# A gated recurrence block on one core: mirrored groups of keys in every second chunk, and the recurrence's last steps behind the bank adds

## The chip, the cores and the metric

The kernel runs on one core of a Trainium2 chip. The metric is the device time of one execution in microseconds, the median of several runs. The engines are named as in the profile: PE is TensorE, DVE is VectorE, ACT is ScalarE, POOL is GpSimd, SP is SyncE, which issues most of the DMAs.

## The reference, cut to what matters

One decoder block on 1024 tokens of width 1024 in float32. A projection gives the queries, the forget gates f, the values, output gates, a pooling branch and merge gates. The part that the change touches is the recurrence, with 8 heads of width 128:

```python
# S_t = diag(f_t) S_{t-1} + k_t v_t^T,  o_t = S_t^T q_t,  k_t = 1 - f_t
scores = einsum('td,sd->ts', q_dec, k_inv);  scores = where(causal, scores, 0)
o_intra = einsum('ts,sv->tv', scores, v)
o_inter = einsum('td,dv->tv', q_dec, state)
state   = decay * state + einsum('sd,sv->dv', k_to_end, v)
```

Its output is normed, gated and projected, merged with the pooling branch, and two layer norms and a squared-ReLU MLP follow. The sum over key tokens s stands in `o_intra` and in the new state, so an order of the keys changes neither, as long as scores, values and decayed keys have the same one.

## The kernel before, in words

All large products are built from 512 x 512 blocks. `pair` computes one block of weights against both token halves with seven products in place of eight (p1 to p7); each product is 12 matmuls of 512 columns (`prod`: high and low parts of weights and activations, lines 213, 215 and 216) into a PSUM bank `ps_pj`. A finished bank is copied out by ACT (`copied`, line 294) or added to an earlier result by DVE (`added`, line 298, the **bank add**). A bank serves a later product only when it has been read. The weights of each product are split into two parts by ACT (line 250) and DVE (line 251).

The tokens of a head are worked in two halves of 512 tokens, and a half in 4 chunks of 128 tokens. A half (`Half`) goes through `prepare` (DVE, ACT and POOL: cumulative decays by scans, then queries and keys scaled in several ways), `turn_keys` (transposes of the decayed keys `ke`, tile `tC`), `scores`, `far_queries`, `states` and `outputs`. `recurrence` is a generator that runs these steps, one or a few between two products of the projections: `PER_HALF` = 8.25 products to a half. The order of TensorE's instructions is thus written by hand; the orders of DVE, ACT, POOL and SP are made by a scheduler that plans with estimated times, so that they can shift wherever an instruction or an order edge changes. `issue_after` puts the instructions of a `with` block behind a named instruction of the same engine.

`scores` fills the tile `sc`, 128 key tokens (partitions) by 4 x 128 query tokens. A chunk's keys stand in four groups of 32, and every matmul has 32 keys as its weights, so it writes 32 partitions: group b writes partitions 32b to 32b + 31, here called quarter 32b. There are three kinds: 4 **diagonal** matmuls to a chunk (`sc<-tF,tD`, 32 columns), 2 **near** ones (`sc<-q,tE`, groups 2 and 0 against the next group of queries, 32 columns) and 2 **far** ones (`sc<-q,k`, groups 0 and 1 against the last 64 queries). The far ones read `q64` and `k64`, each of which is half an ACT copy (lines 1057 and 1060) and half a DVE product (lines 1058 and 1061). The causal part of `sc` is copied into `att` under the mask `cmask` (line 1089). The other DVE steps of `prepare` that the text names are `q` and `tE` by `T` (lines 1049 and 1050) and `ke`, which is `tC<-tE,ek` (line 1052).

The values are computed early and stored to DRAM by `put` (line 554), 128 tokens by 512 columns at a time; `values` loads them for each half.

Of the kernel before, what the change touches and what calls it, by code (L numbers as in the profile page):

```python
# [22 lines left out]
HALF = 512  # L23
CH = HALF // P
SUB = 16
NB = HALF // SUB
# [26 lines left out]
def tile_hybrid_block(  # L53
# [18 lines left out]
    nc = tc.nc  # L72
    V, A, G, PE = nc.vector, nc.scalar, nc.gpsimd, nc.tensor
# [5 lines left out]
    const = ctx.enter_context(tc.tile_pool(name="const", bufs=1))  # L79
# [51 lines left out]
    def split_into(t, src):  # L131
# [3 lines left out]

    ident = const.tile([P, P], F32, name="ident")
    make_identity(nc, ident)
    cmask = const.tile([P, P], F32, name="cmask")
    G.memset(cmask, 1.0)
    G.affine_select(  # L140
        out=cmask, in_=cmask, compare_op=ALU.is_ge, fill=0.0, base=0,
        pattern=[[1, P]], channel_multiplier=-1,
    )
# [99 lines left out]
    def w_tile():  # L243
        return wq.tile([P, CH, P], F32R, tag="w", name=nm("w"), bufs=NW)

    hi_of, lo_of, last_act = [], [], [None]

    def w_part(src):
        hi, lo = w_tile(), w_tile()
# [13 lines left out]

    def behind_act():
        return tc.issue_after(last_act[0])

    n_c = [0]

# [17 lines left out]
    def pair(raw, rooms, takes, pz_tag="pj", twin=False, pc_tag="pj", turned=False):  # L286


        b11, b12, b21, b22, t = raw if len(raw) == 5 else (*raw, None)
        c, ps = {}, {}  # L290

        def copied(room, ps):
            t = room()
            noted(A.copy(t, ps))  # L294
            return t

        def added(t, ps):
            V.tensor_add(t, t, ps)  # L298
            return t

        def make_t3():
            c["t"] = block_tile() if t is None else t
            V.tensor_sub(c["t"], b22, b12)  # L303

        def t3():
            if twin:
                make_t3()
            return w_part(c["t"])

        def t2():  # L310
            if not twin:
                make_t3()
                make_t2()
            return w_part(b12)

        def make_t2():
            if turned:
                minus_sum(b12, c["t"], b11)
            else:
                V.tensor_add(b12, c["t"], b11)  # L320

        def t4():
            if twin:
                make_t2()
            if turned:
                minus_sum(b21, b12, b21)
            else:
                V.tensor_sub(b21, b21, b12)
            return w_part(b21)

        def t1():
            if turned:
                minus_sum(c["t"], b22, b12)
            else:
                V.tensor_sub(c["t"], b22, b12)
            return w_part(c["t"])

        def p1(w):
            ps["a"] = ps_tile()
            prod(ps["a"], w, "a11", True)  # L340
            c[11] = copied(rooms[0], ps["a"])

        def p2(w):
            if pz_tag == "pj":
                ps["z"] = ps_tile()
            ps["c"] = ps_tile(pc_tag, 4 if pc_tag == "pj" else 2)
            prod(ps["c"], w, "a12", True)

        def p7(w):
            if pz_tag != "pj":  # L350
                ps["z"] = ps_tile(pz_tag, 2)
            prod(ps["z"], w, "s3", True)
            with tc.high_priority(PRIO):
                takes[0](added(c[11], ps["c"]))
                c[22] = copied(rooms[2], ps["z"])

        def p6(w):
            prod(ps["a"], w, "s2", False)
            with tc.high_priority(PRIO):
                c[21] = copied(rooms[1], ps["a"])  # L360
                if twin:
                    takes[2](added(c[21], ps["z"]))

        def p4(w):
            prod(ps["z"], w, "a22", False)
            if not twin:
                with tc.high_priority(PRIO):
                    takes[2](added(c[21], ps["z"]))

        def p5(w):  # L370
            prod(ps["a"], w, "s1", False)
            with tc.high_priority(PRIO):
                takes[3](added(c[22], ps["a"]))

        def p3(w):
            prod(ps["a"], w, "s4", False)
# [81 lines left out]
    vd = [[dram(f"v{u}_{nh}", CH * HALF) for nh in range(2)] for u in range(2)]  # L458
    ca = ctx.enter_context(tc.tile_pool(name="ca", bufs=4, reuse_waits="tile"))
    wq = w_scope.enter_context(tc.tile_pool(name="wq", bufs=1, side="right", reuse_waits="tile"))  # L460
    with tc.tile_pool(name="xr", bufs=8, side="right", reuse_waits="tile") as xr:
# [5 lines left out]
        ps = ps_tile("hg", 2)  # L467
# [83 lines left out]
                    take(c, ps)  # L551

        def put(u, nh, c, t):
            nc.sync.dma_start(out=vd[u][nh].rearrange("p (c d) -> p c d", d=HALF)[:, c], in_=t)

        c11, c21, c22 = ([None] * CH for _ in range(3))
        taken = {}
# [184 lines left out]
    with tc.tile_pool(name="tmp", bufs=1, side="right", reuse_waits="tile") as tmp:  # L742
# [227 lines left out]
        def pairs_of(t):  # L970
            return t.rearrange("p (b e s) -> p b e s", e=2, s=SUB)

        def half64(t, e):
            return t.rearrange("p (c e b s) -> p c e b s", e=2, b=2, s=2 * SUB)[:, :, e]

        def bc(a, shape):
            return a.unsqueeze(len(a.shape)).to_broadcast(shape)

        def chunk(c):
            return slice(c * P, (c + 1) * P)  # L980

        def b32(t):
            return t.rearrange("p (b s) -> p b s", s=32)

        class Half:
# [4 lines left out]
            def prepare(self):  # L990

                h, u = self.h, self.u
# [15 lines left out]
                rT = small("rT", [P, NB])  # L1008
                V.reciprocal(rT, blk(fd)[:, :, SUB - 1])
                rT2 = rT.rearrange("p (b e) -> p b e", e=2)  # L1010
                T = small("T", [P, NB])
# [21 lines left out]
                V.tensor_mul(q, q, fd)  # L1033
                k = ft
                with behind_act():
                    A.activation(k, ft, AF.Identity, bias=cmask[:, P - 1 : P], scale=-1.0)
                self.kr = kr = tt("tE")
                V.tensor_mul(kr, k, to_end)
                yield
# [9 lines left out]
                V.tensor_mul(pairs_of(q)[:, :, 1], pairs_of(q)[:, :, 1], bc(T2[:, :, 0], [P, NB // 2, SUB]))  # L1049
                V.tensor_mul(pairs_of(kr)[:, :, 0], pairs_of(kr)[:, :, 0], bc(T2[:, :, 1], [P, NB // 2, SUB]))  # L1050
                self.ke = ke = to_end
                V.tensor_mul(b32(ke), b32(kr), bc(ek.rearrange("p c b -> p (c b)"), [P, 16, 32]))
                yield
                self.q64 = q64 = hgp.tile([P, CH, 2, 32], F32, tag="q64", name=nm("q64"))
                self.k64 = k64 = hgp.tile([P, CH, 2, 32], F32, tag="k64", name=nm("k64"))
                with behind_act():
                    A.copy(q64[:, :, 0], half64(q, 1)[:, :, 0])
                V.tensor_mul(q64[:, :, 1], half64(q, 1)[:, :, 1], bc(p32[:, :, 2], [P, CH, 32]))
                with behind_act():
                    A.copy(k64[:, :, 1], half64(kr, 0)[:, :, 1])  # L1060
                V.tensor_mul(k64[:, :, 0], half64(kr, 0)[:, :, 0], bc(p32[:, :, 1], [P, CH, 32]))
                self.q = q

            def turn_keys(self):
# [8 lines left out]
            def scores(self):  # L1073

                def score(part, lo, keys, queries):
                    PE.matmul(sc[part : part + 32, lo : lo + queries.shape[-1]], keys, queries, start=True, stop=True)
# [12 lines left out]
                V.copy_predicated(  # L1089
                    att, cmask.bitcast(U32).unsqueeze(1).to_broadcast([P, CH, P]),  # L1090
                    sc.rearrange("p (c t) -> p c t", t=P),
                )

            def far_queries(self):
# [565 lines left out]
```

## Time and profile before

| | |
|---|---|
| median of 3 runs | 1442.57 us (1440.68 to 1442.67) |
| profiled execution | 1440.68 us; span from first to last instruction 1439.0 us |
| granted TensorE clock | 0.998 |
| busy: PE, DVE, ACT, POOL | 1424.9, 1099.3, 753.6, 108.6 us |
| blocks of scores (tile `sc`) | 16, the first at 136.8 us, the last until 547 us |
| mean DMA traffic | 159 GB/s |

In rows of the timeline the columns are start in us, length in us, engine, line, operation, output<-inputs, shape and count; what ended an idle time before the row stands in brackets. A row by tile gives the shortest, median and longest duration in ns. Matmuls overlap, so their lengths are not to be summed: what counts is the step from one start to the next.

### The profile page before, as it was taken

The numbers are of one execution on the slowest core, as the hardware profiler recorded it, in microseconds if no ns is written. First come the engines' busy times: TensorE is split into PE (matmuls) and PEld (weight loads), VectorE is DVE, ScalarE is ACT, GpSimd is POOL, SyncE is SP. The second block draws the span as 40 slices with busy tenths as digits, with TensorE's granted clock in tenths as the row PEclk, the third lists the DMA queues.
The fourth block names the chain that finished last, engine by engine and source line by source line (L and its number), as shares of the span: only waits on it lengthen the run. The fifth ranks groups of instructions, "written<-read, shape, count | busy, mean of one in ns | idle before, by whom it ended". The sixth has DMA issues, their size and how long they took to land.

```text
span 1439.0 us, 21137 instructions
## 1 busy us (share of the span) xinstructions
PE 1424.9 (99%) x7499; PEld 1184.6 (82%) x7499; DVE 1099.3 (76%) x1816; ACT 753.6 (52%) x1376; POOL 108.6 (8%) x296
## 2 busy tenths in 40 slices
PE   9999999999999999999999999999999999999997
PEld 7888888888888888878888888888888888888886
DVE  5967887897797796579965697666666787777978
ACT  5445566666656655456532375555556443433534
POOL 0002011111211210100003000000000100000000
PEclk9999999999999999999999999999999999999999
DMA  7142254444454546799651225444456864444422
GB/s 271 62 137 91 87 131 148 109 128 145 110 125 132 142 124 189 214 325 348 190 205 64 99 66 189 155 161 161 149 180 245 292 243 146 149 141 167 133 73 117
DMA packets 186794, 228.17 MB, mean 159 GB/s; under 512 B 12192, under 2 KB 110784, under 8 KB 186688
## 3 DMA queue, kind: packets, MB, share of 16 engines
q1 hardware_dynamic: 180080, 210.94, 44.0%
q0 software_dynamic: 5824, 13.63, 4.5%
q10 hardware_dynamic: 784, 2.25, 0.5%
q8 instruction: 59, 0.97, 0.3%
q14 instruction: 47, 0.39, 0.1%
HBM read 149.70 MB, written 77.07 MB: 158 GB/s over the span
## 4 chain that ended last, share of the span: by engine, by line
PE 94%; DVE 3%; DMA 1%; issue 1%; ACT 1%; DVEq 0%; POOL 0%; ACTq 0%; SPq 0%; POOLq 0%
PE ps_pj L213 16%; PE ps_pj L215 16%; PE ps_pj L216 16%; PE ps_pj L1539 4%; PE ps_pj L1538 4%; PE ps_pj L1537 4%; PE ps_pj L115 2%; PE ps_pj L116 2%; PE ps_pj L114 2%; PE ps_tr L1539 2%; PE ps_tr L1538 2%; PE ps_tr L1537 2%; PE ps_hg L216 1%; PE ps_sc L213 1%; PE ps_sc L216 1%; PE ps_hg L213 1%
## 5 line engine op out<-in xcount | busy, mean ns | idle before, releaser
L213 PE MATMUL ps_pj<-act,w 128*128 128x512 f32 x1068 | 420.1, 393 | 2.7 <-DVE c L298 2.4
L215 PE MATMUL ps_pj<-act,w 128*128 128x512 f32 x1068 | 415.4, 389 | 0.0
L216 PE MATMUL ps_pj<-act,w 128*128 128x512 f32 x1068 | 415.1, 389 | 0.0
L250 ACT CAST w<-raw 128x512 fp32r<-128x512 f32 x303 | 187.7, 621 | 260.6 <-PE ps_pj L215 179.9
L251 DVE TENSOR_TENSOR w<-raw,w 128x512 fp32r<-128x512 f32 x303 | 207.1, 686 | 95.8 <-ACT w L250 93.3
L213 PEld LDWEIGHTS ps_pj<-act,w 128*128 128x128 f32 x1068 | 200.6, 188 | 46.1 <-DVE c L298 3.7
L216 PEld LDWEIGHTS ps_pj<-act,w 128*128 128x128 f32 x1068 | 200.5, 188 | 42.2
L215 PEld LDWEIGHTS ps_pj<-act,w 128*128 128x128 f32 x1068 | 200.6, 188 | 40.4
L1499 ACT CAST act<-act 128x1024 fp32r<-128x1024 f32 x66 | 67.1, 1050 | 108.4 <-issue 35.0
L1538 PE MATMUL ps_pj<-act,act 128*128 128x512 f32 x240 | 93.1, 389 | 0.0
L1539 PE MATMUL ps_pj<-act,act 128*128 128x512 f32 x240 | 93.1, 389 | 0.0
L1500 DVE TENSOR_TENSOR act<-act,act 128x1024 fp32r<-128x1024 f32 x66 | 79.4, 1219 | 17.4 <-ACT act L1499 17.4
L1537 PE MATMUL ps_pj<-act,act 128*128 128x512 f32 x240 | 92.6, 389 | 0.0
L298 DVE TENSOR_TENSOR c<-c,ps_pj 128x512 f32<-128x512 f32 x91 | 62.1, 683 | 33.4 <-PE ps_pj L216 32.3
L294 ACT COPY c<-ps_pj 128x512 f32<-128x512 f32 x92 | 53.3, 581 | 3.3 <-PE ps_pj L216 1.8
L1538 PEld LDWEIGHTS ps_pj<-act,act 128*128 128x128 f32 x240 | 45.1, 188 | 9.5 <-DVE act L1500 0.2
L1537 PEld LDWEIGHTS ps_pj<-act,act 128*128 128x128 f32 x240 | 45.1, 188 | 9.4
L1539 PEld LDWEIGHTS ps_pj<-act,act 128*128 128x128 f32 x240 | 45.1, 188 | 9.3
L303 DVE TENSOR_TENSOR raw<-raw,raw 128x512 f32<-128x512 f32 x43 | 29.6, 688 | 24.6 <-DMA raw<-in_w_in_dram 19.7
L1408 ACT ACTIVATE c<-c 128x512 f32<-128x512 f32 x61 | 38.5, 633 | 1.7
L1407 ACT ACTIVATE c<-c 128x512 f32<-128x512 f32 x46 | 29.0, 632 | 16.3 <-DVE c L298 16.3
L737 POOL DMA_DIRECT2D s<-og x28 | 24.9, 1162 | 137.1 <-DVE og L1150 137.1
(432 smaller groups left out, 2706.4 us busy)
## 6 DMA issues: line engine op xcount, KB each, us to landing
h<-c SPq DMA_DIRECT2D x106, 256.0 KB, 2.9
raw<-in_w_in_dram SPq DMA_DIRECT2D x100, 256.0 KB, 3.3
act<-h SPq DMA_DIRECT2D x78, 256.0 KB, 2.9
draw<-in_w_down_dram SPq DMA_DIRECT2D x16, 1024.0 KB, 8.2
raw<-in_w_up_dram SPq DMA_DIRECT2D x56, 256.0 KB, 2.9
hf<-h SPq DMA_DIRECT2D x34, 256.0 KB, 2.9
s<-og POOLq DMA_DIRECT2D x28, 256.0 KB, 6.0
v<-v SPq DMA_DIRECT2D x16, 256.0 KB, 3.4
```

Source lines behind the costliest of these rows:

```text
L213: PE.matmul(ps, wh[:, k], th, start=first and k == 0, stop=False, skip_group_check=True)
L215: PE.matmul(ps, wh[:, k], tl, start=False, stop=False, skip_group_check=True)
L216: PE.matmul(ps, wl[:, k], th, start=False, stop=k == CH - 1, skip_group_check=True)
L250: hi_of.append(A.copy(hi, src).ins)
L251: lo_of.append(V.tensor_sub(lo, src, f(hi)).ins)
L294: noted(A.copy(t, ps))
L298: V.tensor_add(t, t, ps)
L1499: A.copy(hi, src)
L1500: V.tensor_sub(lo, src, f(hi))
L1537: PE.matmul(ps, hh[:, w], wh, start=fresh and n == 0, stop=False, skip_group_check=True)
L1538: PE.matmul(ps, hh[:, w], wl, start=False, stop=False, skip_group_check=True)
L1539: PE.matmul(ps, hl[:, w], wh, start=False, stop=n == M - 1, skip_group_check=True)
```

## The change

The keys of chunks 1 and 3 of each half stand in mirrored order of their four groups of 32 (3, 2, 1, 0). Three places follow suit: the quarter of `sc` that a group's matmul writes (`place`), the values in DRAM (`put` stores an odd chunk by four DMAs of 32 tokens), and `ke`, which is now made by one DVE instruction for the even chunks and one, with reversed groups, for the odd ones. `cmask` gets a second mask for the odd chunks. In `scores` all near matmuls now come ahead of all far ones. Two small tiles, `rT` and `T`, have one buffer and not two. And in `prepare` the DVE steps on `q`, `kr` (`tE`), `ke`, `q64` and `k64` are put behind the latest bank add (`behind_add`).

```diff
-    cmask = const.tile([P, P], F32, name="cmask")
+    cmask = const.tile([P, 2, P], F32, name="cmask")
     G.memset(cmask, 1.0)
...
+    for b in range(4):
+        part = cmask[b * 32 : (b + 1) * 32, 1]
+        G.affine_select(
+            out=part, in_=part, compare_op=ALU.is_ge, fill=0.0, base=-32 * (3 - b),
+            pattern=[[1, P]], channel_multiplier=-1,
+        )
...
+    def behind_add():
+        return tc.issue_after(last_add[0])
...
         def added(t, ps):
-            V.tensor_add(t, t, ps)
+            last_add[0] = V.tensor_add(t, t, ps).ins
             return t
...
         def put(u, nh, c, t):
-            nc.sync.dma_start(out=vd[u][nh].rearrange("p (c d) -> p c d", d=HALF)[:, c], in_=t)
+            to = vd[u][nh].rearrange("p (c d) -> p c d", d=HALF)[:, c]
+            if c % 2 == 0:
+                nc.sync.dma_start(out=to, in_=t)
+            else:
+                for b in range(4):
+                    nc.sync.dma_start(out=to[(3 - b) * 32 : (4 - b) * 32], in_=t[b * 32 : (b + 1) * 32])
...
-                V.tensor_mul(pairs_of(q)[:, :, 1], pairs_of(q)[:, :, 1], bc(T2[:, :, 0], [P, NB // 2, SUB]))
-                V.tensor_mul(pairs_of(kr)[:, :, 0], pairs_of(kr)[:, :, 0], bc(T2[:, :, 1], [P, NB // 2, SUB]))
-                self.ke = ke = to_end
-                V.tensor_mul(b32(ke), b32(kr), bc(ek.rearrange("p c b -> p (c b)"), [P, 16, 32]))
+                with behind_add():
+                    V.tensor_mul(pairs_of(q)[:, :, 1], pairs_of(q)[:, :, 1], bc(T2[:, :, 0], [P, NB // 2, SUB]))
+                    V.tensor_mul(pairs_of(kr)[:, :, 0], pairs_of(kr)[:, :, 0], bc(T2[:, :, 1], [P, NB // 2, SUB]))
+                    self.ke = ke = to_end
+                    for e in range(2):
+                        order = slice(None, None, -1) if e else slice(None)
+                        V.tensor_mul(
+                            by_chunk(ke)[:, :, e], by_chunk(kr)[:, :, e, order],
+                            bc(ek.rearrange("p (c e) b -> p c e b", e=2)[:, :, e, order], [P, 2, 4, 32]),
+                        )
                 yield
...
                 with behind_act():
                     A.copy(q64[:, :, 0], half64(q, 1)[:, :, 0])
-                V.tensor_mul(q64[:, :, 1], half64(q, 1)[:, :, 1], bc(p32[:, :, 2], [P, CH, 32]))
-                with behind_act():
                     A.copy(k64[:, :, 1], half64(kr, 0)[:, :, 1])
-                V.tensor_mul(k64[:, :, 0], half64(kr, 0)[:, :, 0], bc(p32[:, :, 1], [P, CH, 32]))
+                with behind_add():
+                    V.tensor_mul(q64[:, :, 1], half64(q, 1)[:, :, 1], bc(p32[:, :, 2], [P, CH, 32]))
+                    V.tensor_mul(k64[:, :, 0], half64(kr, 0)[:, :, 0], bc(p32[:, :, 1], [P, CH, 32]))
...
+                def place(c, b):
+                    return 32 * (3 - b if c % 2 else b)
+
                 for c in range(CH):
                     for b in range(4):
                         lo = c * P + b * 32
-                        score(b * 32, lo, self.kc[:, lo : lo + 32], self.qc[:, lo : lo + 32])
+                        score(place(c, b), lo, self.kc[:, lo : lo + 32], self.qc[:, lo : lo + 32])
+                for c in range(CH):
+                    for b in (0, 2):
+                        lo = c * P + b * 32
+                        score(place(c, b), lo + 32, self.kr[:, lo : lo + 32], self.q[:, lo + 32 : lo + 64])
                 for c in range(CH):
                     far = self.q64[:, c].rearrange("p a b -> p (a b)")
                     for b in range(2):
-                        score(b * 32, c * P + 64, self.k64[:, c, b], far)
-                    for b in (2, 0):
-                        lo = c * P + b * 32
-                        score(b * 32, lo + 32, self.kr[:, lo : lo + 32], self.q[:, lo + 32 : lo + 64])
+                        score(place(c, b), c * P + 64, self.k64[:, c, b], far)
```

**TensorE, the first block of scores.** The rows give line, operation, output<-inputs, output shape and count; `ps_tr` takes the turned keys, `tF,tD` are the diagonal operands, `q,k` the far and `q,tE` the near ones. Before, the last two rows come four times in turn, once for a chunk:

```order
L216 MATMUL ps_pj_1408<-act_301,w_1383 128x512
L1069 MATMUL ps_tr_1421<-ident,tC_1212 128x128 x4
L1076 MATMUL sc<-tF_1303,tD_1300 32x32 x16
L1076 MATMUL sc<-q_202_1348,k_203_1349 32x64 x2
L1076 MATMUL sc<-q_1108,tE_1276 32x32 x2
```

The same place now:

```order
L222 MATMUL ps_pj_1437<-act_305,w_1412 128x512
L1092 MATMUL ps_tr_1450<-ident,tC_1240 128x128 x4
L1099 MATMUL sc<-tF_1331,tD_1328 32x32 x16
L1099 MATMUL sc<-q_1136,tE_1304 32x32 x8
L1099 MATMUL sc<-q_202_1377,k_203_1378 32x64 x8
```

The same 32 matmuls stand in the block, with the near ones in one row of eight ahead of the far ones; nothing else moves on TensorE in the whole program.

**VectorE, the bank add at 400.9 us of the trace** (`c<-c,ps_pj`; `raw` is a sum of weight blocks, `pA` and `pC` are pooling steps). Before:

```order
L1050 TENSOR_TENSOR tE_4356<-tE_4356,T_4316 128x16x16
L328 TENSOR_TENSOR raw_4501<-raw_4501,raw_4504 128x512
L1049 TENSOR_TENSOR q_4142<-q_4142,T_4316 128x16x16
L917 TENSOR_TENSOR pA_4425<-pC_4423 128x265
L1052 TENSOR_TENSOR tC_4291<-tE_4356,ek_4329 128x512
L1061 TENSOR_TENSOR k_809_4494<-tE_4356,p_770_4318 128x4x32
L298 TENSOR_TENSOR c_4431<-c_4431,ps_pj_4297 128x512
```

Now:

```order
L337 TENSOR_TENSOR raw_4540<-raw_4540,raw_4543 128x512
L931 TENSOR_TENSOR pA_4463<-pC_4461 128x265
L307 TENSOR_TENSOR c_4469<-c_4469,ps_pj_4335 128x512
L1067 TENSOR_TENSOR q_4179<-q_4179,T_4354 128x16x16
L936 TENSOR_TENSOR pA_4463<-pA_4463,inv_n 128x7
L938 SCALAR_TENSOR_TENSOR c_4348<-pA_4463,c_4348 128x249
L1068 TENSOR_TENSOR tE_4394<-tE_4394,T_4354 128x16x16
L257 TENSOR_TENSOR w_4691<-raw_4543,w_4690 128x512
L1123 TENSOR_TENSOR tA_4677<-q_4179,eq_4362 128x512
L937 TENSOR_TENSOR c_4348<-pA_4463,c_4348 128x7
L1072 TENSOR_TENSOR tC_4329<-tE_4394,ek_4367 128x2x128 x2
```

The add stands ahead of the steps on `tE`, `q`, `tC` and `k64`, which came before it; `q64` and `k64` come after the next bank add, which follows these rows.

**VectorE, the bank add at 540.3 us of the trace.** Before:

```order
L1050 TENSOR_TENSOR tE_6026<-tE_6026,T_5986 128x16x16
L1049 TENSOR_TENSOR q_5323<-q_5323,T_5986 128x16x16
L328 TENSOR_TENSOR raw_6146<-raw_6146,raw_6149 128x512
L922 TENSOR_TENSOR pC_5927<-pC_5927,inv_n 128x15
L924 SCALAR_TENSOR_TENSOR c_5908<-pC_5927,c_5908 128x241
L917 TENSOR_TENSOR pA_5933<-c_5761 128x271
L1052 TENSOR_TENSOR tC_5961<-tE_6026,ek_5999 128x512
L298 TENSOR_TENSOR c_6088<-c_6088,ps_pj_5967 128x512
```

Now:

```order
L337 TENSOR_TENSOR raw_6190<-raw_6190,raw_6193 128x512
L931 TENSOR_TENSOR pC_5970<-pA_5968 128x257
L307 TENSOR_TENSOR c_6131<-c_6131,ps_pj_6010 128x512
L1067 TENSOR_TENSOR q_5364<-q_5364,T_6029 128x16x16
L1068 TENSOR_TENSOR tE_6069<-tE_6069,T_6029 128x16x16
L936 TENSOR_TENSOR pC_5970<-pC_5970,inv_n 128x15
L938 SCALAR_TENSOR_TENSOR c_5951<-pC_5970,c_5951 128x241
L931 TENSOR_TENSOR pA_5976<-c_5804 128x271
```

Here too the steps on `tE`, `q` and `tC`, and three pooling steps with them, have moved behind the add.

More of the change, by code (lines that the diff above doesn't have):

```diff
@@ L137, in tile_hybrid_block @@
     make_identity(nc, ident)
-    cmask = const.tile([P, P], F32, name="cmask")
+    cmask = const.tile([P, 2, P], F32, name="cmask")
     G.memset(cmask, 1.0)
     G.affine_select(
-        out=cmask, in_=cmask, compare_op=ALU.is_ge, fill=0.0, base=0,
+        out=cmask[:, 0], in_=cmask[:, 0], compare_op=ALU.is_ge, fill=0.0, base=0,
         pattern=[[1, P]], channel_multiplier=-1,
     )
+    for b in range(4):
[4 more added lines that the diff above has]
+        )
     eps_rms = const.tile([P, 1], F32, name="eps_rms")
@@ L244, in w_tile @@
         return wq.tile([P, CH, P], F32R, tag="w", name=nm("w"), bufs=NW)
-    hi_of, lo_of, last_act = [], [], [None]
+    hi_of, lo_of, last_act, last_add = [], [], [None], [None]
     def w_part(src):
@@ L980, in chunk, with by_chunk @@
             return slice(c * P, (c + 1) * P)
+        def by_chunk(t):
+            return t.rearrange("p (c e b s) -> p c e b s", e=2, b=4, s=32)
         def b32(t):
@@ L1007, in prepare @@
                 )
-                rT = small("rT", [P, NB])
+                rT = small("rT", [P, NB], 1)
                 V.reciprocal(rT, blk(fd)[:, :, SUB - 1])
                 rT2 = rT.rearrange("p (b e) -> p b e", e=2)
-                T = small("T", [P, NB])
+                T = small("T", [P, NB], 1)
                 G.tensor_copy(T, blk(fd)[:, :, SUB - 1])
@@ L1035, in prepare @@
                 with behind_act():
-                    A.activation(k, ft, AF.Identity, bias=cmask[:, P - 1 : P], scale=-1.0)
+                    A.activation(k, ft, AF.Identity, bias=cmask[:, 0, P - 1 : P], scale=-1.0)
                 self.kr = kr = tt("tE")
@@ L1084, in scores @@
                     for b in range(2):
-                        score(b * 32, c * P + 64, self.k64[:, c, b], far)
-                    for b in (2, 0):
-                        lo = c * P + b * 32
-                        score(b * 32, lo + 32, self.kr[:, lo : lo + 32], self.q[:, lo + 32 : lo + 64])
+                        score(place(c, b), c * P + 64, self.k64[:, c, b], far)
                 V.copy_predicated(
-                    att, cmask.bitcast(U32).unsqueeze(1).to_broadcast([P, CH, P]),
-                    sc.rearrange("p (c t) -> p c t", t=P),
+                    att.rearrange("p (c e) t -> p c e t", e=2), cmask.bitcast(U32).unsqueeze(1).to_broadcast([P, 2, 2, P]),
+                    sc.rearrange("p (c e t) -> p c e t", e=2, t=P),
                 )
```

## The prediction

> **What bounds the kernel now.** I read the page first: the share of each engine and the chain that ended last.
>
> ```profile
> PE 1424.9 (99%) x7499; PEld 1184.6 (82%) x7499; DVE 1099.3 (76%) x1816; ACT 753.6 (52%) x1376; POOL 108.6 (8%) x296
> PE 94%; DVE 3%; DMA 1%; issue 1%; ACT 1%; DVEq 0%; POOL 0%; ACTq 0%; SPq 0%; POOLq 0%
> ```
>
> TensorE is never out of work for long, and the chain is 94% its own. So the time is TensorE's own stream plus its few stops, and another engine counts only where TensorE waits for it. Next, the stops: the chain of waits of TensorE, whose largest entry is the one the change can touch, and the load of VectorE in the later half of the recurrence.
>
> ```profile
> PE ps_pj L213 <- DVE c L298: 2.4, 2, 1.4
> 400.00:547.00 147.00, 144.61 (x1072) 121.80 (x1070) 128.88 (x277) 88.39 (x207) 26.98 (x76) 1.00 0.50 132
> ```
>
> Two stops, 2.4 us together, end with a bank add (L298) on VectorE, which is busy 128.88 of 147.00 us there (88%). Then the small matmuls that the change reorders, by tile (`sc`), and one block of them in the timeline:
>
> ```profile
> L1076 PE MATMUL sc<-tF,tD x512: 196/196/217, 136.8 to 546.1; 128*32 128x32 f32 x171
> L1076 PE MATMUL sc<-q,k x256: 219/220/243, 137.1 to 546.7; 128*32 128x64 f32 x128
> L1076 PE MATMUL sc<-q,tE x256: 192/196/218, 137.1 to 546.8; 128*32 128x32 f32 x128
> 136.79 0.46 PE L1076 MATMUL sc<-tF,tD 128*32 128x32 f32 x32
> ...
> 137.35 0.19 PE L1076 MATMUL sc<-q,tE 128*32 128x32 f32 x1
> 137.36 0.24 PE L1076 MATMUL sc<-q,k 128*32 128x64 f32 x1
> 137.36 0.22 PE L1076 MATMUL sc<-q,tE 128*32 128x32 f32 x2
> 137.41 0.22 PE L1076 MATMUL sc<-q,k 128*32 128x64 f32 x1
> 137.42 0.20 PE L1076 MATMUL sc<-q,tE 128*32 128x32 f32 x1
> 137.44 0.25 PE L1076 MATMUL sc<-q,k 128*32 128x64 f32 x2
> 137.53 0.19 PE L1076 MATMUL sc<-q,tE 128*32 128x32 f32 x1
> ...
> 137.70 0.22 PE L1076 MATMUL sc<-q,tE 128*32 128x32 f32 x2
> 137.86 0.50 PE L213 MATMUL ps_pj<-act,w 128*128 128x512 f32 x1
> ```
>
> There are 16 such blocks, one for each head and half. A block has 16 diagonal, 8 near (`q,tE`) and 8 far (`q,k`) matmuls, and the counts of 512, 256 and 256 say that each leaves two records. A block holds TensorE from 136.79 to 137.86, 1.07 us. The 32 diagonal records go round the four quarters of the output partitions (0, 32, 64, 96). Their last start is at 0.46 - 0.196 = 0.264 us, so a record starts every 8.2 ns though each lasts 196: four quarters work side by side, and a quarter is held about 4 x 8.2 = 33 ns by one record of 32 columns.
>
> The far and near records instead repeat every 0.175 us (137.35, 137.53, 137.70), with 8 records to a period: one chunk of 128 tokens. By the code a chunk's far pair goes to quarters 0 and 32, its near pair to 64 and 0. Quarter 0 thus takes one far and one near matmul in every chunk, 64 and 32 one each, 96 none. If the period is quarter 0's, a far record holds it (175 - 2 x 33) / 2 = 54.5 ns, which is plausible beside 33 for half its columns. So this part of the block is bound by one quarter of the array: 4 x 0.175 = 0.70 us.
>
> **Part 1, the scores.** After the change odd chunks are mirrored: their near pair goes to quarters 96 and 32, their far pair to 96 and 64. Over two chunks every quarter gets exactly one near and one far matmul, 2 x 33 + 2 x 54.5 = 175 ns. Four chunks take 0.35 us where they took 0.70: 0.35 saved. Near first and far last means that the block ends on a 54.5 ns record and not on one of 33: 0.02 back. The diagonal part has a cost too: mirrored, the quarters run 0, 32, 64, 96, 96, 64, 32, 0 and so on, so that the same quarter follows itself at three chunk boundaries. Bounds: nothing, if later matmuls pass a held one; 3 x 2 x 33 = 0.20 us, if each boundary waits for both records of a matmul. The timeline above decides for the low end: the program has four far records and then four near ones in each chunk, but the starts come as near, far, near, near, far, near, far, far, so quarters do pass each other. I take 0.02. A block saves 0.31 us, between 0.13 and 0.35, and 16 blocks save **5.0 us**, between 2.1 and 5.6.
>
> The row speaks against a rule of the Trainium skill: "TensorE: Matmul & The Clock Gate", Part 3 (Packing small matmuls), says that matmuls start and end strictly in program order. By that rule the sum for this part would be about zero (rival 2).
>
> **Part 2, the order on VectorE.** Here are the two stops, TensorE's rows and VectorE's:
>
> ```profile
> 400.34 0.39 PE L216 MATMUL ps_pj<-act,w 128*128 128x512 f32 x1
> 401.67 0.50 PE L213 MATMUL ps_pj<-act,w 128*128 128x512 f32 x1 [0.94 <-DVE c L298]
> 398.52 0.41 DVE L1050 TENSOR_TENSOR tE<-tE,T 128x256 f32<-128x256 f32 x1
> 398.85 0.68 DVE L328 TENSOR_TENSOR raw<-raw,raw 128x512 f32<-128x512 f32 x1
> 399.45 0.41 DVE L1049 TENSOR_TENSOR q<-q,T 128x256 f32<-128x256 f32 x1
> ...
> 400.14 0.68 DVE L1052 TENSOR_TENSOR tC<-tE,ek 128x512 f32<-128x512 f32 x1
> 400.74 0.28 DVE L1061 TENSOR_TENSOR k<-tE,p 128x128 f32<-128x128 f32 x1
> 400.94 0.67 DVE L298 TENSOR_TENSOR c<-c,ps_pj 128x512 f32<-128x512 f32 x1
> 538.94 0.39 PE L215 MATMUL ps_pj<-act,w 128*128 128x512 f32 x1
> 539.17 0.39 PE L216 MATMUL ps_pj<-act,w 128*128 128x512 f32 x1
> 541.00 0.50 PE L213 MATMUL ps_pj<-act,w 128*128 128x512 f32 x1 [1.44 <-DVE c L298]
> 537.63 0.42 DVE L1050 TENSOR_TENSOR tE<-tE,T 128x256 f32<-128x256 f32 x1
> 537.97 0.42 DVE L1049 TENSOR_TENSOR q<-q,T 128x256 f32<-128x256 f32 x1
> 538.30 0.68 DVE L328 TENSOR_TENSOR raw<-raw,raw 128x512 f32<-128x512 f32 x1
> 538.91 0.17 DVE L922 TENSOR_TENSOR pC<-pC,inv_n 128x15 f32<-128x15 f32 x1
> ...
> 539.66 0.68 DVE L1052 TENSOR_TENSOR tC<-tE,ek 128x512 f32<-128x512 f32 x1
> 540.27 0.68 DVE L298 TENSOR_TENSOR c<-c,ps_pj 128x512 f32<-128x512 f32 x1
> ```
>
> Matmuls of 512 columns start every 0.23 us (538.94, 539.17). So the first stop costs 401.67 - 400.34 - 0.23 = 1.10 us, the second 541.00 - 539.17 - 0.23 = 1.60. Neither add waits for its product: between that product's last matmul and the stopped L213 stand the 12 matmuls of another product, 2.7 us; the add stands behind VectorE's own backlog. In the new order four of the recurrence's steps stand behind the first add: tE (398.85 - 398.52 = 0.33), q (399.79 by the 0.34 that its kind takes there), tC (0.60) and k (0.20), together 1.47 us. The add would start at 399.47 and be over by 400.14, ahead of 400.34 + 0.23 = 400.57. At the second, tE, q, the pooling steps from 538.91 to 539.66 and tC move behind: 0.34 + 0.33 + 0.75 + 0.61 = 2.03 us. The add ends at 540.95 - 2.03 = 538.92, ahead of 539.40. Both stops go, with 0.4 to 0.5 us to spare: **2.7 us**. What is late next there is nothing for TensorE until the next bank. A third, smaller one goes the same way, since one step of `q` moves behind its add:
>
> ```profile
> 127.48 0.39 PE L216 MATMUL ps_pj<-act,w 128*128 128x512 f32 x1
> 127.95 0.50 PE L213 MATMUL ps_pj<-act,w 128*128 128x512 f32 x1
> ```
>
> 0.47 - 0.23 = 0.24 us, against 0.33 moved. I count 0.2. Bounds of this part: 0, if the backlog reappears at other adds, and 2.9.
>
> **What is added beside TensorE.** The decayed keys tC are made in two halves: twice 0.34 (a step of 256 elements) instead of 0.60, so 0.08 x 16 = 1.3 us more on VectorE, hidden as long as TensorE does not wait for it. 8 of the 16 value stores become four each. A store's issue takes 0.32 us on SyncE:
>
> ```profile
> L554 SPq DMA_DIRECT2D v<-c x8: 320/332/437, 29.7 to 95.5; - x8
> L554 SPq DMA_DIRECT2D v<-x x8: 319/319/339, 70.1 to 82.8; - x8
> ```
>
> 24 more make 7.7 us of issue between 30 and 97 us, about 1 us at each of 8 places, and the loads of the first weight blocks (`raw`, L224) queue behind them. No stop of TensorE in that stretch ends with a load, and the values are first read behind the first block of scores (136.79), so I count 0; if that cover is missing, a late weight block costs 1 us once or twice. Four more selects and two single-buffered tiles on GpSimd: 0, GpSimd is 8% busy and idle between halves.
>
> Sum: 5.0 + 2.7 + 0.2 = 7.9 us. The profiled execution (1440.68 us, span 1439.0) would become 1432.8. It was the fastest of the three runs; against the median of 1442.57 the forecast is 1434.7.
>
> **Rivals.** (1) Only the scores gain; VectorE, with 1.3 us more and TensorE 0.3 us earlier in every half, is as late at other adds as it was at these. For it: 88% busy. Against: both streaks gain 1.5 to 2.0 us of room and need 1.1 and 1.6. Time 1442.57 - 5.0 = 1437.6.
>
> (2) The change does not do what it says on TensorE: starts are in order. Then a far matmul takes its two records one after the other whatever quarter is next: 8 x 54.5 + 8 x 33 = 0.70 us, as now. Against: in order, the 16 diagonal matmuls would take 16 x 33 = 0.53 us to start, and they take 0.264. Time 1442.57 - 2.9 = 1439.7.
>
> (3) Slower: the late steps of the keys. Two multiplies that feed the far matmuls (q64, k64), and tC for the transposes, now stand in VectorE's queue behind a bank add, which cannot start before its product's last matmul; the ScalarE copies that complete q64 and k64 stand behind the same add's readers. TensorE, in order, would stop in the middle of a block. The tightest half before:
>
> ```profile
> 487.62 0.30 ACT L1060 COPY k<-tE 128x128 f32<-128x128 f32 x1
> 488.92 0.25 PE L1076 MATMUL sc<-q,k 128*32 128x64 f32 x2
> ```
>
> The spare is 488.92 - 487.92 = 1.0 us; an add one product late (12 x 0.23 = 2.7) costs 1.7. In 5 of 16 halves that eats the gain; in 8 it is 13.6 us, and the time 1442.57 - 7.9 + 13.6 = 1448.3. Against: in the new order the far matmuls come last in the block, 0.13 us later than now, and the adds in front of them are of products that ended some us before.
>
> **How the numbers follow.** Forecast 0.70; rival 1 0.13; rival 2 0.06; rival 3 0.06; 0.05 for the early loads and smaller losses together. The forecast's own range: parts 1 and 2 between 4.0 + 2.0 and 5.6 + 2.9, so 1434.1 to 1436.6; the runs shown lie up to 1.9 us below their median, which takes it down to 1432.5. Rival 1 brings the upper end, with a little for the early loads: 1438.4. The measurement can tell about 0.2% (2.9 us) from no change: 1439.7 and 1445.5 are the marks. Forecast and rival 1 are faster, rival 2 sits on the mark: faster 0.89, same 0.05, slower 0.06.
>
> **What would show it.** The block of `sc` should last 0.74 to 0.80 us from its first record to the next L213, and its near and far records should start at an even 8 and 14 ns and not in periods of 175. The wait of L213 for L298's successor should be gone from TensorE's list. Wrong would be: blocks still near 1.07 (rival 2), new stops at bank adds (1), a stop inside a block, or in front of the transposes of tC, ended by VectorE or ScalarE (3).

## The result, and the profile after

| | before | after |
|---|---|---|
| median | 1442.19 us (20 runs) | 1435.37 us (20 runs) |
| profiled execution, span | 1440.68, 1439.0 us | 1434.66, 1433.0 us |

The ratio of the times is 0.9958, with a 95% interval of 0.995 to 0.9965: 6.1 us faster by the ratio, 6.8 by the medians, 6.0 between the two profiled executions, where 7.9 were forecast. One execution of experiment B below ran at a granted clock of 0.556 and took 2408.94 us; no ratio includes it.

The engines' busy time on the page, after:

```profile
PE 1420.8 (99%) x7499; PEld 1180.1 (82%) x7499; DVE 1099.2 (77%) x1832; ACT 753.2 (53%) x1376; POOL 110.9 (8%) x300
```

The list of TensorE's waits, after (us in total, times, longest):

```profile
PE ps_hg L480 <- POOL ident masks.py:199: 1.8, 1, 1.8
PE ps_tr L114 <- DVE f L905: 1.4, 1, 1.4
PE ps_tr L177 <- DVE x L204: 0.7, 1, 0.7
PE ps_sc L538 <- DVE c L580: 0.5, 1, 0.5
PE ps_pj L219 <- ACT c L303: 0.2, 1, 0.2
```

The entry that led the list before, 2.4 us of the bank add (now line 307), is gone, and VectorE does the same work in the same time. What has grown is the wait for `f` (L905), from 0.7 to 1.4 us. The two places of the former stops in TensorE's timeline, the matmuls that waited being those at 398.02 and 535.19:

```profile
397.80 0.39 PE L222 MATMUL ps_pj<-act,w 128*128 128x512 f32 x1
398.02 0.39 PE L219 MATMUL ps_pj<-act,w 128*128 128x512 f32 x1
...
534.96 0.39 PE L222 MATMUL ps_pj<-act,w 128*128 128x512 f32 x1
535.19 0.39 PE L219 MATMUL ps_pj<-act,w 128*128 128x512 f32 x1
```

And in VectorE's:

```profile
396.92 0.67 DVE L307 TENSOR_TENSOR c<-c,ps_pj 128x512 f32<-128x512 f32 x1
397.51 0.41 DVE L1067 TENSOR_TENSOR q<-q,T 128x256 f32<-128x256 f32 x1
...
533.44 0.68 DVE L307 TENSOR_TENSOR c<-c,ps_pj 128x512 f32<-128x512 f32 x1
```

Both start 0.22 to 0.23 us behind their predecessors, the usual step. The first add ends at 397.59, 0.43 us ahead of its matmul, the second at 534.12, 1.07 us ahead. `q` (L1067) now follows the add. The small stop near 128 us is gone as well.

The first block of scores, and the one at 217 us (timeline of TensorE):

```profile
136.33 0.46 PE L1099 MATMUL sc<-tF,tD 128*32 128x32 f32 x32
136.60 0.37 PE L1099 MATMUL sc<-q,tE 128*32 128x32 f32 x16
136.82 0.43 PE L1099 MATMUL sc<-q,k 128*32 128x64 f32 x16
137.19 0.50 PE L219 MATMUL ps_pj<-act,w 128*128 128x512 f32 x1
...
217.04 0.46 PE L1099 MATMUL sc<-tF,tD 128*32 128x32 f32 x32
217.32 0.34 PE L1099 MATMUL sc<-q,tE 128*32 128x32 f32 x14
217.46 0.24 PE L1099 MATMUL sc<-q,k 128*32 128x64 f32 x1
217.48 0.21 PE L1099 MATMUL sc<-q,tE 128*32 128x32 f32 x2
217.51 0.41 PE L1099 MATMUL sc<-q,k 128*32 128x64 f32 x15
217.85 0.50 PE L219 MATMUL ps_pj<-act,w 128*128 128x512 f32 x1
```

From its first record to the next L219 a block takes 0.86 us, in 15 of 16 blocks; the one at 217 us takes 0.81. So a block is 0.21 us shorter than before, not 0.31. The 32 diagonal records take 0.27 us as they did: the reversed quarters cost nothing. The 16 near records take from 136.60 to the last start at 136.60 + 0.37 - 0.196 = 136.77, 11.6 ns each where 8.2 were expected. Then 15 blocks have a gap of about 0.05 us before the far records, and the block at 217 us has none: its first far record starts among the near ones. In the trace 15 blocks have a semaphore instruction (a wait that stands as an instruction of its own) of 51 ns on TensorE's queue between the near and the far group, and the block at 217 us has none. Before, 12 blocks have one behind the diagonal group, and all 16 take 1.07 us with it or without. The rows of these instructions, before and after (shortest, median and longest in ns):

```profile
L1076 PEldq EVENT_SEMAPHORE  x12: 51/51/51, 136.9 to 545.9; - x12
...
L1099 PEldq EVENT_SEMAPHORE  x15: 51/51/51, 136.7 to 540.3; - x15
```

So the sum of the prediction came out like this, from the steps between starts in the two traces: blocks 16 x 0.21 = 3.4 us; the three stops 2.9, and 0.4 more because the matmul behind a stop starts 0.34 us after it and not 0.23, and some later ones a little late; given back 0.5 at the waits for `f` and 0.6 in two small stops at 465 and 491 us, counted in the same way. The first matmul's start, 0.11 us later than before, is made up by 6.94 us of the trace. That is 5.6 of 6.0 us.

### The profile page after: what moved, and what is told of

It is laid out like the page before. It is cut to its first block, busy times and chain, and to the rows that moved or that the text cites. A ratio compares the mean times of both kernels' runs of the same rounds, so it can differ in the third digit from the quotient of the medians.

```text
span 1433.0 us, 21208 instructions
## 1 busy us (share of the span) xinstructions
PE 1420.8 (99%) x7499; PEld 1180.1 (82%) x7499; DVE 1099.2 (77%) x1832; ACT 753.2 (53%) x1376; POOL 110.9 (8%) x300
## 4 chain that ended last, share of the span: by engine, by line
PE 95%; DVE 2%; DMA 1%; ACT 1%; issue 1%; POOL 0%; DVEq 0%; ACTq 0%; SPq 0%; POOLq 0%
PE ps_pj L219 16%; PE ps_pj L222 16%; PE ps_pj L221 16%; PE ps_pj L1565 4%; PE ps_pj L1566 4%; PE ps_pj L1564 4%; PE ps_pj L115 2%; PE ps_pj L114 2%; PE ps_pj L116 2%; PE ps_tr L1566 2%; PE ps_tr L1565 2%; PE ps_tr L1564 2%; PE ps_hg L219 1%; PE ps_sc L219 1%; PE ps_sc L222 1%; PE ps_hg L221 1%
## 5 line engine op out<-in xcount | busy, mean ns | idle before, releaser
L219 PE MATMUL ps_pj<-act,w 128*128 128x512 f32 x1068 | 419.9, 393 | 0.3 <-ACT c L303 0.2
L219 PEld LDWEIGHTS ps_pj<-act,w 128*128 128x128 f32 x1068 | 200.5, 188 | 44.1 <-ACT c L303 1.3
```

Of the source, the lines that this page charges most:

```text
L219: PE.matmul(ps, wh[:, k], th, start=first and k == 0, stop=False, skip_group_check=True)
```

## The experiments

Each kernel was compared with the kernel before on the same chip: A to D on one chip, E to H on a second, I to K on a third. D, F, G and I had a single profiled run.

**A, the scores alone**: the changed kernel without the new order on VectorE (the copy for `k64` stands behind `q64`'s product again, as before).

```diff
 def behind_add():
-    return tc.issue_after(last_add[0])
+    return nullcontext()
```

> The reversed chunks and the near-first, far-last order alone; VectorE's steps stand in the old order among the bank adds. Theory (the two parts add up; a block of scores is 0.21 us shorter): blocks of 0.86 us instead of 1.07, 16 x 0.21 = 3.4 us faster than before, with the stops of 1.1 and 1.6 us at the bank adds still there. Rival (the shorter block only lets TensorE arrive earlier at bank adds that are late anyway): blocks of 0.86 us, but the two stops grow by up to 3.4 us together and the gain is under 1.5 us.

Ratio 0.997 (0.9958 to 0.9982), 4.3 us (2.6 to 6.1). Twelve blocks took 0.86 us or a little more, four 0.81. One entry of TensorE's waits:

```profile
PE ps_pj L219 <- DVE c L307: 2.0, 3, 1.0
```

The stops at bank adds are there, three instead of two (1.0, 0.5 and 0.5 us) and no larger together than before, so the shorter blocks were not swallowed by them. The theory holds.

**B, the adds alone**: the kernel before with `behind_add` around the same steps, and the two small tiles with one buffer.

> The recurrence's last steps behind the bank adds alone; keys in their old order, scores chunk by chunk. Theory: blocks stay at 1.07 us, the stops of 1.1, 1.6 and 0.24 us go, 2.5 to 2.9 us faster than before. Rival (the backlog of VectorE shows up at other adds, or the far matmuls, which stand first in their chunk here, wait for the late q64 and k64): under 1 us faster, with new stops at adds or inside blocks.

Ratio 0.998 (0.9971 to 0.999), 2.9 us. All blocks but two stayed at 1.07 us and the bank-add entry shrank from 2.4 to 0.3 us. But a stop appeared inside one block, the mechanism of the prediction's third rival (timeline of TensorE):

```profile
487.95 0.44 PE L1080 MATMUL sc<-q,k 128*32 128x64 f32 x3 [1.18 <-ACT q L1061]
```

That block took 2.55 us, so B's gain is what was left of a larger one. A and B together give 7.2 us by their ratios, against 6.1 for the whole change (5.0 to 7.2): two parts that add up, as far as this can be told.

**C, far first**: in the changed kernel the loop over far pairs ahead of that over near pairs.

> The changed kernel with the far matmuls ahead of the near ones, behind the diagonal ones. Theory (the wait for the keys of the far pairs costs 50 ns because it stands between two short groups; ahead of the far group it is read while the diagonal group still runs; the near records need 11 ns each in any place): blocks of 0.79 to 0.81 us, 16 x 0.05 = 0.8 us faster than the changed kernel. Second theory (the near records are slow only because they follow the diagonal ones; behind the far ones they start every 8.2 ns): blocks of 0.74 to 0.77 us, 1.4 to 1.9 us faster than the changed kernel. Rival (the far keys are not ready yet so early and stop TensorE inside the block): blocks of 0.9 us and more in some halves, no gain.

Ratio 0.9958 (0.9946 to 0.997), the same as the change. TensorE's timeline, the first block and the stop in the one at 483 us:

```profile
135.97 0.46 PE L1099 MATMUL sc<-tF,tD 128*32 128x32 f32 x32
136.24 0.43 PE L1099 MATMUL sc<-q,k 128*32 128x64 f32 x15
...
136.50 0.32 PE L1099 MATMUL sc<-q,tE 128*32 128x32 f32 x15
136.75 0.50 PE L219 MATMUL ps_pj<-act,w 128*128 128x512 f32 x1
...
484.60 0.57 PE L1099 MATMUL sc<-q,k 128*32 128x64 f32 x13 [0.90 <-ACT q L1080]
```

ScalarE ahead of that stop:

```profile
482.73 0.63 ACT L839 ACTIVATE c<-c 128x512 f32<-128x512 f32 x1 [6.32 <-DVE c L307]
...
484.25 0.30 ACT L1080 COPY q<-q 128x128 f32<-128x128 f32 x1
```

Fifteen blocks take 0.78 us, between the two theories, 0.08 less than in the changed kernel; the gap ahead of the far records is gone, and the near ones need 9.8 ns. The 1.2 us of that went into a stop of the rival's kind, but in one half only, whose block took 2.04 us: the copy that completes `q64` (L1080) stands on ScalarE behind a gate (L839) that waits for a bank add, while ScalarE was idle for 6.32 us. Why that add was late shows under K.

**D, the order alone**: the kernel before, no chunk reversed, near first and far last.

> The kernel before with near first and far last, and no chunk reversed: near pairs all in quarters 0 and 64, far pairs all in quarters 0 and 32, VectorE as before. Theory (a quarter of the output partitions is held by a record, 33 ns for 32 columns and 54.5 for 64, and the groups run one after the other): near 8 x 33 = 0.26 us with two quarters at work, far 8 x 54.5 = 0.44 us, no shorter than the 0.70 of before; blocks of 1.07 to 1.13 us. Rival (the order alone makes the block short, whatever the quarters): blocks of 0.86 us as in the changed kernel.

TensorE's timeline:

```profile
135.89 0.46 PE L1076 MATMUL sc<-tF,tD 128*32 128x32 f32 x32
136.16 0.39 PE L1076 MATMUL sc<-q,tE 128*32 128x32 f32 x13
...
136.96 0.50 PE L213 MATMUL ps_pj<-act,w 128*128 128x512 f32 x1
```

Thirteen blocks of 1.07 us, none shorter; 1444.05 us in its one run. That time holds more stops than before (8.9 against 6.2 us in all), among them one in the block at 488 us, which took 2.87 us:

```profile
490.64 0.83 PE L1076 MATMUL sc<-q,k 128*32 128x64 f32 x16 [1.39 <-ACT q L1057]
```

So the lengths of the blocks decide here, not the time: the order without the reversal gains nothing. Twelve blocks have the semaphore instruction, here behind 48 records, and the undisturbed ones take 1.07 us with it or without.

**E, far first and early copies**: C, with ScalarE's copies for `q64` and `k64` not held back.

```diff
-with behind_act():
-    A.copy(q64[:, :, 0], half64(q, 1)[:, :, 0])
-    A.copy(k64[:, :, 1], half64(kr, 0)[:, :, 1])
+A.copy(q64[:, :, 0], half64(q, 1)[:, :, 0])
+A.copy(k64[:, :, 1], half64(kr, 0)[:, :, 1])
```

> Far matmuls ahead of the near ones, and ScalarE's two copies that complete the far pairs no longer held behind its last bank copy. Theory (the stop of 0.9 us in the half at 483 us comes from those copies standing behind a gate that waits for a bank add): all 16 blocks are 0.78 us and that stop is gone; what of it is gained depends on the bank add near 491 us, which was the next stop (0.66 us) and takes up what TensorE gains in front of it, so 0 to 1.2 us faster than with the copies held back. Rival (the copies now stand ahead of weight casts on ScalarE and delay them by 0.4 us in every half): new stops at weights, no faster or slower than the changed kernel.

Ratio 0.9937 (0.9925 to 0.995), 1431.86 us. The changed kernel once more, on the same chip (**H**):

> The changed kernel as it is, on the same chip as the versions beside it, so that they can be compared: 6 to 8 us faster than before, blocks of 0.86 us, one of 0.81.

Ratio 0.9957 (0.9943 to 0.997), 1434.4 us. So E was 2.5 us faster than the change by the medians; the intervals meet at their edges. All its blocks but the last were 0.78 us, the stop at 483 was gone, and so was the wait for the bank add near 491. No stop at a weight appeared.

**F, near, diagonal, far**: the near loop moved ahead of the diagonal one.

> The changed kernel with the near matmuls ahead of the diagonal ones, and the far ones last. Theory (the 50 ns are the reading of a second semaphore in front of the far group, which costs nothing while a long group is still running): the diagonal group of 0.26 us stands in front of it, no gap ahead of the far records, blocks of 0.77 to 0.80 us. Rival (the gap comes with the change from 32 to 64 columns, or the near records are slow in any place): blocks of 0.84 us or more.

TensorE's timeline, the first block and the one at 217 us, which again has no semaphore instruction:

```profile
136.09 0.33 PE L1099 MATMUL sc<-q,tE 128*32 128x32 f32 x16
136.24 0.48 PE L1099 MATMUL sc<-tF,tD 128*32 128x32 f32 x32
136.59 0.43 PE L1099 MATMUL sc<-q,k 128*32 128x64 f32 x16
136.95 0.50 PE L219 MATMUL ps_pj<-act,w 128*128 128x512 f32 x1
...
216.83 0.33 PE L1099 MATMUL sc<-q,tE 128*32 128x32 f32 x16
...
217.62 0.50 PE L219 MATMUL ps_pj<-act,w 128*128 128x512 f32 x1
...
485.86 0.62 PE L1099 MATMUL sc<-q,k 128*32 128x64 f32 x16 [1.22 <-ACT q L1080]
```

Most blocks took 0.84 us and the one without the instruction 0.79. The last row is a stop for the copy of `q64`, as in C and D; its block took 2.40 us, and it stands in the run's 1437.48 us. The theory of this run fell: the long diagonal group in front did not hide the instruction. But the records say why. The near ones, now first, have their last start 0.33 - 0.196 = 0.134 us after the first, which is where the 16th diagonal record starts in the other versions; the diagonal ones, now records 17 to 48, went on in the same steps as far as the 32nd record of the block and at about 10.6 ns from there. So it is the place that slows a record, from the 33rd on, not its kind, and where the quarters are evenly loaded the semaphore instruction costs its 50 ns when it stands behind 48 records. In the kernel before and in C it stands behind 32, is read 0.10 to 0.14 us after the block's start, and costs nothing.

**G, the reversal alone**: chunks reversed, the old order in each, far pair and then near pair.

> The changed kernel's reversed chunks with the old order in each chunk, far pair and then near pair. Theory (only the load of the quarters counts, records pass each other freely): two chunks still give each quarter one near and one far matmul, blocks of 0.78 to 0.80 us. Rival (records pass each other only within a short window, so that the quarter that a chunk uses twice still sets the pace): the period of a chunk stays near 0.13 to 0.175 us and blocks are 0.90 to 1.07 us.

TensorE's timeline:

```profile
136.79 0.46 PE L1099 MATMUL sc<-tF,tD 128*32 128x32 f32 x32
137.06 0.25 PE L1099 MATMUL sc<-q,k 128*32 128x64 f32 x2
...
137.58 0.50 PE L219 MATMUL ps_pj<-act,w 128*128 128x512 f32 x1
```

Fifteen blocks of 0.80 us and one of 1.30, 1433.62 us in its one run. With D this settles the part on the scores: the gain comes from the load of the quarters, 0.27 us a block. The reordering of near and far, taken by itself, cost 0.06 us of it in each block, nearly all since it moved the semaphore instruction behind 48 records (I).

**I, one semaphore**: the changed kernel with the two copies on VectorE, so that the far matmuls wait for VectorE only.

```diff
-with behind_act():
-    A.copy(q64[:, :, 0], half64(q, 1)[:, :, 0])
-    A.copy(k64[:, :, 1], half64(kr, 0)[:, :, 1])
 with behind_add():
+    V.tensor_copy(q64[:, :, 0], half64(q, 1)[:, :, 0])
+    V.tensor_copy(k64[:, :, 1], half64(kr, 0)[:, :, 1])
```

> The changed kernel with its order of matmuls (diagonal, near, far), and the two copies that complete q64 and k64 moved from ScalarE to VectorE, so that the far matmuls wait for one engine and TensorE's queue holds no semaphore instruction in front of them. Theory (that instruction costs 50 ns in 15 of 16 blocks because it stands behind 24 matmuls, where the queue is no longer far ahead): all blocks 0.80 to 0.81 us, as the one block without it had. Rival (the gap in front of the far records has another cause, the readiness of the keys among them): blocks stay at 0.86 us in 15 halves. Time: VectorE has 6 us more to do, so new stops at bank adds are possible; 0.8 us faster than the changed kernel without them.

TensorE's timeline:

```profile
135.98 0.46 PE L1098 MATMUL sc<-tF,tD 128*32 128x32 f32 x32
136.25 0.34 PE L1098 MATMUL sc<-q,tE 128*32 128x32 f32 x14
136.40 0.24 PE L1098 MATMUL sc<-q,k 128*32 128x64 f32 x1
...
136.78 0.50 PE L219 MATMUL ps_pj<-act,w 128*128 128x512 f32 x1
```

Fourteen blocks of 0.81 us; the two others were stretched by short stops. The instruction is the 50 ns. The time (1435.24 us, one run) did not gain: there is a bank-add wait of 1.0 us near 492. VectorE's larger load was expected to give such waits, but the repeat of E has one of the same length near 491 without that load, so the cause is not shown.

**J, early copies alone**, and **K, reversal with the old order and early copies**, on one chip:

> The changed kernel with its order of matmuls, and ScalarE's two copies not held behind its last bank copy. Theory (those copies cost a stop only where the block is shorter and reaches them earlier; the changed kernel has no stop there): blocks of 0.86 us, 0 to 1 us faster than the changed kernel, and 1.2 us or more slower than with the far matmuls first as well. Rival (the early copies are what makes the version with both faster): 2 to 3 us faster than the changed kernel.

> Reversed chunks, the old order in each chunk (far pair, then near pair), the late steps behind the bank adds, ScalarE's copies not held. Theory (only the load of the quarters and the place of the semaphore count): blocks of 0.796 us without a stop inside them, no wait at the bank adds near 400 and 540 us, 9 to 11 us faster than before, within 0.5 us of the version with all far matmuls first. Rival (bank adds near 491 us are late whatever the copies do): a stop of 0.7 us stays there and the gain is 8 to 9 us.

J: ratio 0.9949 (0.9936 to 0.9962), about 1 us faster than the change and 1 to 2 us slower than E, differences within the intervals, at the theory's end of its expectation. Its blocks were not all 0.86 us: six took 0.81, those in which the semaphore instruction was missing. K: 0.9944 (0.9932 to 0.9956), 8.1 us, with blocks of 0.80 us but for one, short of its theory and in the range of its rival; its profile has stops near 484 and 494 us. Where they come from shows at a step of VectorE that adds two weight blocks. In E:

```profile
476.75 0.69 DVE L312 TENSOR_TENSOR raw<-raw,raw 128x512 f32<-128x512 f32 x1 [2.81 <-DMA raw<-in_w_in_dram]
```

In K:

```profile
481.82 0.69 DVE L312 TENSOR_TENSOR raw<-raw,raw 128x512 f32<-128x512 f32 x1 [6.98 <-DMA raw<-in_w_in_dram]
```

And TensorE's stops behind it in K:

```profile
484.26 0.69 PE L1091 MATMUL ps_tr<-ident,tC 128*128 128x128 f32 x3 [0.86 <-DVE tC L1072]
486.96 0.50 PE L219 MATMUL ps_pj<-act,w 128*128 128x512 f32 x1 [0.80 <-ACT c L303]
493.69 0.50 PE L219 MATMUL ps_pj<-act,w 128*128 128x512 f32 x1 [0.98 <-DVE c L307]
```

VectorE stands until a load of `raw` has landed, and the recurrence's last steps and the bank add queue behind it; ScalarE's gate and, where they are held, the copies for `q64` and `k64` come after that add. In the versions with both parts of the change, between 483 and 495 us, TensorE was not idle with that step at 476.75 and 478.37 us (E, H), 0.1 us with it at 478.87 (the changed kernel's profile), 0.7 at 479.05 (G), 1.4 at 479.26 (C), 1.1 at 479.84 (I), and 1.9, 1.8 and 2.9 at 480.51, 481.47 and 481.82 (F, J, K). So the stops of C and F in this stretch go with the load as well, and K's rival, that the add near 491 is late whatever the copies do, fits K but not E.

**E once more**, on another chip:

> The version with the far matmuls first and the copies not held, once more, on another chip. Theory (its gain over the changed kernel is its blocks, 16 x 0.077 = 1.2 us, and stops between 483 and 495 us whose size depends on when the weight load issued near 469 us lands): ratio to before 0.993 to 0.996; in the profile blocks of 0.78 us, and stops between 483 and 495 us only if VectorE waits for that load until after 480 us. Rival (the copies held no longer are a gain of 2.5 us by themselves): 0.9925 to 0.994 again, with no stop there whenever the load lands.

Ratio 0.9945 (0.9931 to 0.9959), 1432.61 us. Its profiled execution had the load's step at 479.44 us, blocks of 0.78 us but for one of 1.03, and 1.2 us of idle time between 483 and 495 us, 1.0 of it at the bank add near 491. So the limit of 480 us was set a little too high, and the rival falls: the same program has that stop or not, and the landing of the load goes with it in these two executions. Why the load lands when it does was not tried. E is the fastest version that was run more than once, 8 to 9 us faster than before and about 2 us faster than the change; the intervals of its second run and of the change overlap.

## Why the prediction came out right

**The scores, mechanism right, term too large.** The reading that one quarter of the array sets the pace is shown by D and G: the order alone leaves 1.07 us, the reversal alone gives 0.80. Two terms of the block's 0.31 us were mis-sized. The first is "Four chunks take 0.35 us where they took 0.70": the even load gained 0.27 us and not 0.35 (G). Once no quarter is overloaded, the records from the 33rd of the block on do not start every 0.35 / 32 = 10.9 ns but every 12.8 on average (G), so another limit takes over; which one was not tried. The second is "Near first and far last means that the block ends on a 54.5 ns record: 0.02 back": that order cost 0.06, because the semaphore instruction for the far pairs comes to stand behind 48 records and takes 0.05 there (F, I). The reversed diagonal costs 0, in place of the 0.02 taken and the 0.20 feared. So a block saves 0.27 - 0.06 = 0.21 us, and the term measured 3.4 us instead of 5.0, inside its bounds of 2.1 and 5.6. In the trace before, the cost of the instruction could not be seen: there it stood where it was free.

**Starts in program order** (the second rival) did not come about: a far record starts at 217.46 ahead of near ones at 217.48 that stand before it in the program, and the block is short. The rule of the Trainium skill that the prediction cites ("TensorE: Matmul & The Clock Gate", Part 3), that matmuls start and end strictly in program order, does not hold for these records.

**The two stops** went as worked out, 2.7 us, with 0.43 us to spare at the first (0.4 to 0.5 were forecast) and 1.07 at the second. The third went too. B measures this part alone at 2.9 us (1.4 to 4.2), with the stop in one of its blocks taken off.

**The first rival** was right in direction: new stops appeared at 465 and 491 us, the second at a bank add, but of 0.6 us together. **The third rival** has its mechanism in B, C, D and F, a block that waits for ScalarE's copy, at the very half that the prediction named as the tightest. The prediction argued that far matmuls last would keep it away. D and F have them last and stopped 1.4 and 1.2 us there; VectorE's step behind the load stands 3.2 and 3.5 us ahead of the block in them, and 5.6 us in the change's profile. There both copies were over before the block began:

```profile
484.06 0.30 ACT L1081 COPY k<-tE 128x128 f32<-128x128 f32 x1
484.46 0.46 PE L1099 MATMUL sc<-tF,tD 128*32 128x32 f32 x32
```

So it was not the order of the matmuls that kept the stop away here: the copies were early, and so was the load. That part of the forecast was luck, since the prediction does not mention this load, and its landing moved between two executions of the same program (E and its repeat).

**Beside TensorE**, the longer issue of the value stores cost nothing that the waits show. Not foreseen was the wait for `f` near 618 us, which gave back 0.5 us. It differs between profiles, 0.7 us in C and E, 1.0 in H and 2.2 in the repeat of E, so it need not be the change's doing; what sets it was not tried.

**Small slips** in the working change nothing: 0.264 us from the first to the 32nd start are 31 steps, of 8.5 ns; 1434.1 less 1.9 is 1432.2 and not 1432.5; the tile `rT` is written by VectorE and not by GpSimd.

## What to carry to other kernels

Where small matmuls write 32 partitions each, count the column time that each quarter of the output gets: an overfull quarter set the time here, and permuting the rows of a sum evened it out at no cost that the waits show, since all operands followed. Do not count on the whole of the difference: once the quarters are even, another limit can come first. Ahead of a group of short matmuls, look where the semaphore instructions stand: early in the block they were read while others ran, late in an evenly loaded block they cost their own length. When a stop is removed, look for the load behind the engine that is now next: here the stops that were left went with its landing.

## What the runs showed of the hardware that was not expected

A block's first 32 records, whatever their kind, started at the same moments, 8.5 ns apart on average with four quarters abreast, and those from the 33rd on farther apart, 10 to 15 ns on average of a group where the quarters were evenly loaded. A semaphore instruction of 51 ns on TensorE's queue cost nothing behind 32 records; behind 48 it cost 50 ns where the quarters were evenly loaded (the changed kernel, F) and nothing where they were not (D). The Trainium skill ("TensorE: Matmul & The Clock Gate", the table at its head) gives TensorE's queue a depth of 64. With a weight load to each record (7499 of each on the page of the profile), 32 records are 64 instructions, so the change of pace behind the 32nd record fits a queue that fills while the transposes ahead of the block hold the array; that this is the cause was not tried.
